# Sliding-window attention: 192 score columns per head in pieces that fit the window, in place of 256 columns and a mask

## The chip, the cores and the metric

One core of one Trainium2 chip runs the whole program. The metric is device time in microseconds (us) of one execution, from the first to the last instruction and what lies around it, as median of several executions.

## The reference

A two-layer streaming trunk: layer 0 is a gated linear recurrence with a SwiGLU FFN, layer 1 is attention with a SwiGLU FFN, and between them one shared K/V projection. The change touches the attention alone. There are 1024 prompt frames in chunks of 64, 16 query heads of 64 numbers in 4 groups, and 4 key/value heads. A query chunk sees the two chunks before it and its own, that is 192 keys, and no mask inside them:

```python
def band(a):
    ap = jnp.pad(a, ((0, 0), (WIN_CHUNKS * CHUNK, 0), (0, 0), (0, 0)))
    ...
    return jnp.concatenate([ap[:, j:j + n] for j in range(WIN_CHUNKS + 1)], axis=2)
...
m = jnp.maximum(jnp.max(s, axis=-1, keepdims=True), sink)
p = jnp.exp(s - m)
denom = jnp.sum(p, axis=-1, keepdims=True) + jnp.exp(sink - m)
return jnp.einsum('bnkgqs,bnskd->bnqkgd', p / denom, v.astype(F32))
```

Besides, 32 frames of a running stream see 128 cached keys and their own 32 (160 in all).

## The kernel before

Activations are kept feature-major in three blocks of frames (384, 384 and 288). All dense products (`mm_fm`, L132 to L142, and others like it) are done in three fp32r passes, high by high, high by low and low by high. One such product of 128 output features for one block is 24 matmuls (L141) of 128x128 weights on 384 or 288 columns, each of which the trace shows as one record.

The attention works on units of 128 queries (two chunks, a "tile") of one key/value head g with its 4 query heads (`hh = 2 * pi + pr`): 3 tiles per block, 4 groups, 3 blocks, 36 units. Tile j of 0 to 8 has 28 units with j = 1 to 7, 4 units with j = 0 (there are no keys before it) and 4 units with j = 8, the 32 sample frames. Each unit has three functions:

- `att_s` (L1249 to L1303): scores (L1272) of 128 queries against 256 keys, the four chunks that either of the two query chunks sees, for 4 heads. Operands are fp32, and each call is two matmul records in the trace. The head number pr picks the upper or the lower 64 rows of the array, because both hold 64 features of a head. Then mask products (L1282) in bf16 add a large negative number to the 64 keys that only the other chunk sees. Per half pr there is one PSUM tile `sc` of 2 heads by 256 columns, from a pool of two buffers. After that come row maxima on VectorE (L1285), the sink, the exponentials on ScalarE (L1294, with their sums), the sum's reciprocal, and the products with it: one VectorE instruction for two heads (L1299), one ScalarE instruction for each of the other two (L1302).
- `att_t` (L1305 to L1322): 8 transposes of 128x128 (L1314) through TensorE, 4 heads for each of the two key tiles, into two PSUM tiles `ptp`; ScalarE copies the first to SBUF (L1319), VectorE the second (L1321).
- `att_v` (L1324 to L1335): for each key tile two calls (L1332) of 128 keys by 64 features on 256 columns, added up in the PSUM tile `pav`, the output's upper or lower 64 partitions by pr. ScalarE rounds it to the high part (L1334), VectorE makes the low part (L1335). `ptp` and `pav` share a pool of two buffers.

The loop (L1394 to L1403) writes, for u = 0 to 12 of a block: the scores of unit u, some dense work as filling, then `att_t` and `att_v` of unit u - 1. The filling stands in `plan` (L1371 to L1381): projections of q that are left over in block 0, the output projection of block 0 in block 1, that of block 1 and the rest of block 0's in block 2. Where `plan` has nothing for a u, no dense work stands between: u = 2, 5, 8, 11 in block 0, 0, 5, 10 in block 1, and 4, 10 in block 2. A scheduler orders each engine's instructions at build time, by this order and by when it reckons that operands and buffers are ready; so dense matmuls are drawn forward into gaps, and the PE queue is then fixed. All DMAs are issued by SyncE's queue.

```python
pss = [aps.tile([128, 512], F32, tag="sc", name="sc", bufs=2)...   # L1264
ptp = aps.tile([128, 512], F32, tag="pt", name="ptp", bufs=2)      # L1312
pav = aps.tile([128, 512], F32, tag="pt", name="pav", bufs=2)...   # L1328
```

Of the kernel before, what the change touches and what calls it, by code (L numbers as in the profile page):

```python
# [29 lines left out]
NEG = -1.0e38  # L30
# [29 lines left out]
def build(nc, tc, I, O):  # L60
    ctx = ExitStack()
    mult, add, sub, mn = ALU.mult, ALU.add, ALU.subtract, ALU.min
# [20 lines left out]
    def tmp(bufs=4):  # L83
        return tp.tile([128, 384], F32, tag="tmp", name="tmp", bufs=bufs)
# [35 lines left out]
    ident = cp.tile([128, 128], F32, name="ident")  # L120
# [554 lines left out]
    def run(g):  # L675
        for _ in g or ():
            pass
# [5 lines left out]
    with tc.tile_pool(name="hp", bufs=1) as hp, \  # L683
# [42 lines left out]
        vts, o_raw, ssq, r_o = {}, {}, {}, {}  # L726
# [308 lines left out]
        p1 = p2 = None  # L1035
# [188 lines left out]
    with tc.tile_pool(name="aps", bufs=1, space=PSUM, reuse_waits="tile") as aps:  # L1224
        nsink = ap2.tile([128, 16], F32, name="nsink")
        nc.sync.dma_start(nsink, I["sinks"])
        nc.vector.tensor_scalar(nsink, nsink, -1.0, None, mult)
        mkf = tmp()
        nc.sync.dma_start(mkf, I["mk"])
        mk = ap2.tile([128, 384], BF16, name="mk")  # L1230
        nc.vector.tensor_copy(mk, mkf)
# [10 lines left out]
        def qload():  # L1242
# [3 lines left out]
            nc.sync.dma_start(qt, qds[b, g].rearrange("pi pr hf r t -> (pr hf r) pi t"))  # L1246
            qts[b, g] = qt

        def att_s(b, g, jl):  # L1249
            j = 3 * b + jl  # L1250
            samp = j == 8
            rows = 32 if samp else 128
            qs = slice(jl * 128, jl * 128 + rows)
            kb = kbs[b]
            if samp:
                keys = [(kc, 0, 128), (kb, 384, 32)]
                vals = [(vc, 128), (vts[8], 32)]
                lo, kend = 0, 160
            elif j == 0:
                keys, vals, lo, kend = [(kb, 128, 128)], [(vts[0], 128)], 128, 256  # L1260
            else:
                keys, vals, lo, kend = [(kb, jl * 128, 256)], [(vts[j - 1], 128), (vts[j], 128)], 0, 256
            rm = ap2.tile([128, 4], F32, tag="rm", name="rm", bufs=2)
            pss = [aps.tile([128, 512], F32, tag="sc", name="sc", bufs=2).rearrange("p (h k) -> p h k", h=2)  # L1264
                   for _ in range(2)]

            for pi in range(2):
                off = lo
                for (kt_, k0, n) in keys:
                    for pr in range(2):  # L1270
                        rsl = slice(pr * 64, pr * 64 + 64)
                        nc.tensor.matmul(pss[pr][:rows, pi, off:off + n], qts[b, g][rsl, pi, qs],  # L1272
                                         kt_[rsl, g, k0:k0 + n], start=pi == 0 and off == lo, stop=samp,
                                         skip_group_check=True)
                    off += n
            if not samp:
                for (c0, k0) in ((0, 128), (192, 256)):
                    if c0 < lo:
                        continue
                    for pr in range(2):  # L1280
                        rsl = slice(pr * 64, pr * 64 + 64)
# [10 lines left out]
            P = ap2.tile([128, 4, 256], F32, tag="P", name="P", bufs=2)  # L1292
            for hh in (0, 2, 1, 3):
                nc.scalar.activation(P[:rows, hh, lo:kend], pss[hh % 2][:rows, hh // 2, lo:kend], AF.Exp,  # L1294
                                     bias=ng[:rows, hh:hh + 1], scale=0.125, accum_out=rs[:rows, hh:hh + 1])
# [5 lines left out]
            for hh in (2, 3):  # L1301
                nc.scalar.activation(P[:rows, hh, lo:kend], P[:rows, hh, lo:kend], AF.Copy, scale=rs[:rows, hh:hh + 1])  # L1302
            return dict(b=b, g=g, rows=rows, qs=qs, vals=vals, lo=lo, P=P)  # L1303

        def att_t(c):  # L1305

            rows, P = c["rows"], c["P"]
            N = 4 * rows
            off = c["lo"]
            c["pt"] = []  # L1310
            for i, (vt, n) in enumerate(c["vals"]):
                ptp = aps.tile([128, 512], F32, tag="pt", name="ptp", bufs=2)  # L1312
                for hh in range(4):
                    nc.tensor.transpose(ptp[:n, hh * rows:hh * rows + rows], P[:rows, hh, off:off + n],  # L1314
                                        ident[:rows, :rows])
                off += n
                pts = ap2.tile([128, 512], F32, tag="pts", name="pts", bufs=4)
                if i == 0:
                    nc.scalar.copy(pts[:n, :N], ptp[:n, :N])  # L1319
                else:  # L1320
                    nc.vector.tensor_copy(pts[:n, :N], ptp[:n, :N])  # L1321
                c["pt"].append(pts)  # L1322

        def att_v(c):  # L1324

            rows, g, qs, vals = c["rows"], c["g"], c["qs"], c["vals"]
            oh, ol = os[c["b"]]
            pav = aps.tile([128, 512], F32, tag="pt", name="pav", bufs=2)[:, :2 * rows].rearrange("p (a q) -> p a q", a=2)  # L1328
            for i, ((vt, n), pts) in enumerate(zip(vals, c["pt"])):
                ph = pts[:n, :4 * rows].rearrange("p (pi pr q) -> p pi pr q", pi=2, pr=2)  # L1330
                for pr in range(2):
                    nc.tensor.matmul(pav[pr * 64:pr * 64 + 64], vt[:n, g * 64:g * 64 + 64], ph[:, :, pr, :],  # L1332
                                     start=i == 0, stop=i == len(vals) - 1, skip_group_check=True)
            nc.scalar.copy(oh[:, 2 * g:2 * g + 2, qs], pav)  # L1334
            nc.vector.tensor_tensor(ol[:, 2 * g:2 * g + 2, qs], pav, oh[:, 2 * g:2 * g + 2, qs].bitcast(F32), sub)  # L1335
# [4 lines left out]
        def wq(g):  # L1340
            return wpair("wq", g, scale="mix_pre1")
# [96 lines left out]
def pack(inp):  # L1438
# [35 lines left out]
    mk = np.zeros((128, 384), np.float32)  # L1474
    for r0 in (0, 64):
        mk[r0, 64:128] = 1.0
        mk[r0 + 1, 0:64] = 1.0
        mk[r0, 128:256] = NEG
        mk[r0 + 1, 256:384] = NEG
    A["mk"] = mk  # L1480
# [35 lines left out]
```

## Time and profile before

| what | value |
|---|---|
| median of 3 runs | 2513.05 us (2509.55 to 2516.27) |
| the profiled execution | 2509.75 us, of which the span is 2508.0 us |
| granted TensorE clock, mean over the span | 0.993 of full speed |
| PE busy in the span | 98% |
| the attention units, first score to last value product | about 1495 to 1742 us of the span |

PE is TensorE's matmuls, PEld its weight loads, DVE VectorE, ACT ScalarE, POOL GpSimd, SP SyncE. A matmul's record lasts longer than it holds up the next one, since matmuls are pipelined: how long a group keeps the engine is read from its start to the start of the next group. "x8" counts records that follow each other, and the us ahead of it run from the first start to the last end.

### The profile page before, as it was taken

What the parts mean: (1) busy time and instruction counts of PE and PEld (TensorE: products, weight loads), DVE (VectorE), ACT (ScalarE), POOL (GpSimd) and SP (SyncE); (2) the same over time, 40 slices, a digit from 0 to 9 for tenths busy, and PEclk for the clock granted to TensorE, in tenths of its full rate; (3) what the DMA queues carried; (4) which work ended last, traced back from release to release, by engine and by line L of the source; (5) the groups of instructions that cost most, each with busy time, mean ns of one, the idle gap of its engine ahead of it and who ended that gap; (6) DMA issues with size and microseconds to landing.
All of it is one profiled execution on the core that took longest, in us unless ns stands there. A gap on an engine that the chain in (4) does not pass through costs nothing.

```text
span 2508.0 us, 43904 instructions
## 1 busy us (share of the span) xinstructions
PE 2455.1 (98%) x17124; PEld 2367.2 (94%) x17124; DVE 1707.5 (68%) x3678; ACT 1130.2 (45%) x2467; POOL 243.3 (10%) x476
## 2 busy tenths in 40 slices
PE   7999999999999999999999999999999999999997
PEld 7999998998999999999999997778999999999997
DVE  8888889888876666652468746678876666643466
ACT  6655655656533333342345326677533333341333
POOL 3343233231000000000000211000000000000000
PEclk9999999999999999999999999999999999999999
DMA  5233334443522222252446532233422222242454
GB/s 177 91 102 102 122 105 133 134 136 106 165 71 86 76 77 76 75 173 81 145 145 204 177 123 71 86 117 102 156 74 77 77 77 77 76 168 77 153 168 157
DMA packets 124153, 287.98 MB, mean 115 GB/s; under 512 B 13432, under 2 KB 68632, under 8 KB 123944
## 3 DMA queue, kind: packets, MB, share of 16 engines
q1 hardware_dynamic: 123944, 285.17, 35.0%
q8 instruction: 134, 2.20, 0.4%
q14 instruction: 75, 0.61, 0.1%
HBM read 237.25 MB, written 48.07 MB: 114 GB/s over the span
## 4 chain that ended last, share of the span: by engine, by line
PE 79%; DVE 10%; DMA 5%; ACT 4%; issue 2%; POOL 1%; SPq 0%; DVEq 0%; ACTq 0%; POOLq 0%
PE mm L141 27%; PE mm L507 17%; PE mm L416 15%; PE mm L153 6%; PE c L416 6%; PE sc L1272 2%; DVE wl L103 2%; PE pav L1332 1%; PE ptp L1314 1%; DMA wst<-in_wfo 1%; ACT wh L102 1%; DVE acc L182 1%; DVE wl L99 1%; DMA xl<-g 1%; DMA wst<-in_wk 1%
## 5 line engine op out<-in xcount | busy, mean ns | idle before, releaser
L141 PE MATMUL mm<-xh,wh 128*128 128x384 f32 (+1 forms) x1968 | 630.4, 321 | 10.4 <-ACT xh L220 7.0
L141 PE MATMUL mm<-xh,wl 128*128 128x384 f32 (+1 forms) x1968 | 622.2, 317 | 4.2 <-DVE wl L103 4.2
L141 PE MATMUL mm<-xl,wh 128*128 128x384 f32 (+1 forms) x1968 | 623.2, 317 | 0.2
L102 ACT CAST wh<-wst 128x1024 fp32r<-128x1024 f32 (+1 forms) x301 | 314.3, 1047 | 365.5 <-PE mm L507 196.5
L103 DVE TENSOR_TENSOR wl<-wst,wh 128x1024 fp32r<-128x1024 f32 (+1 forms) x301 | 368.1, 1226 | 137.7 <-ACT wh L102 137.3
L141 PEld LDWEIGHTS mm<-xh,wh 128*128 128x128 f32 x1968 | 371.2, 189 | 19.5 <-ACT xh L220 7.0
L141 PEld LDWEIGHTS mm<-xh,wl 128*128 128x128 f32 x1968 | 371.7, 189 | 10.6 <-DVE wl L103 6.2
L141 PEld LDWEIGHTS mm<-xl,wh 128*128 128x128 f32 x1968 | 371.5, 189 | 8.7 <-issue 5.0
L507 PE MATMUL mm<-xh,wl 128*128 128x384 f32 (+1 forms) x768 | 247.3, 322 | 2.4 <-DVE wl L103 2.4
L507 PE MATMUL mm<-xh,wh 128*128 128x384 f32 (+1 forms) x768 | 247.3, 322 | 0.0
L507 PE MATMUL mm<-xl,wh 128*128 128x384 f32 (+1 forms) x768 | 247.2, 322 | 0.0
L153 PE MATMUL mm<-wh,xh 128*128 128x256 f32 (+1 forms) x648 | 188.1, 290 | 3.9 <-DVE tmp L1130 2.5
L153 PE MATMUL mm<-wh,xl 128*128 128x256 f32 (+1 forms) x648 | 184.5, 285 | 0.0
L153 PE MATMUL mm<-wl,xh 128*128 128x256 f32 (+1 forms) x648 | 184.3, 284 | 0.0
L400 ACT CAST sh<-sr 128x512 fp32r<-128x512 f32 x144 | 89.5, 622 | 173.8 <-PE mm L416 145.6
L507 PEld LDWEIGHTS mm<-xh,wl 128*128 128x128 f32 x768 | 144.9, 189 | 2.8 <-DVE wl L103 2.8
L507 PEld LDWEIGHTS mm<-xl,wh 128*128 128x128 f32 x768 | 144.8, 189 | 0.0
L507 PEld LDWEIGHTS mm<-xh,wh 128*128 128x128 f32 x768 | 144.7, 188 | 0.0
L153 PEld LDWEIGHTS mm<-wh,xh 128*128 128x128 f32 (+1 forms) x648 | 119.2, 184 | 6.7 <-DVE tmp L1130 2.6
L153 PEld LDWEIGHTS mm<-wh,xl 128*128 128x128 f32 (+1 forms) x648 | 119.3, 184 | 0.8 <-issue 0.2
L153 PEld LDWEIGHTS mm<-wl,xh 128*128 128x128 f32 (+1 forms) x648 | 119.5, 184 | 0.6
L399 DVE TENSOR_TENSOR sr<-wst 128x512 f32<-128x512 f32 x72 | 49.5, 688 | 74.9 <-DMA wst<-in_wfi 74.9
(284 smaller groups left out, 5115.7 us busy)
## 6 DMA issues: line engine op xcount, KB each, us to landing
wst<-in_wfo SPq DMA_DIRECT2D x92, 512.0 KB
wst<-in_wfi SPq DMA_DIRECT2D x88, 512.0 KB
wst<-in_wfq SPq DMA_DIRECT2D x47, 512.0 KB
g<-u SPq DMA_DIRECT2D x72, 192.0 KB
wst<-in_wi SPq DMA_DIRECT2D x24, 512.0 KB
wst<-in_wg SPq DMA_DIRECT2D x24, 512.0 KB
wst<-in_wao SPq DMA_DIRECT2D x24, 512.0 KB
xl<-g SPq DMA_DIRECT2D x32, 384.0 KB
```

Of the source, the lines that this page charges most:

```text
L99: nc.vector.scalar_tensor_tensor(wl[:, s], st[:, s], pcol(name, k0 + k), wh[:, s].bitcast(F32), mult, sub)
L102: nc.scalar.copy(wh[:, s], st[:, s])
L103: nc.vector.tensor_tensor(wl[:, s], st[:, s], wh[:, s].bitcast(F32), sub)
L141: last_mm[0] = nc.tensor.matmul(ps[:, :W], w, x, start=i == 0, stop=i == n - 1)
L153: last_mm[0] = nc.tensor.matmul(ps[:rows, :256], x, w, start=i == 0, stop=i == n - 1)
L182: nc.vector.tensor_tensor(acc[:, :W], acc[:, :W], q[:, :W], add)
L399: nc.vector.tensor_tensor(r, x, y, op)
L400: nc.scalar.copy(h, r)
L416: last_mm[0] = nc.tensor.matmul(ps[:, :384], a, c, start=start and k == i == 0, stop=k == 3 and i == 2, skip_group_check=True)
L507: last_mm[0] = nc.tensor.matmul(ps[:, :W], a, c[:, q, :], start=start and q == i == 0, stop=stop and q == f - 1 and i == 2, skip_group_che ...
L1272: nc.tensor.matmul(pss[pr][:rows, pi, off:off + n], qts[b, g][rsl, pi, qs], kt_[rsl, g, k0:k0 + n], start=pi == 0 and off == lo, stop=samp ...
L1314: nc.tensor.transpose(ptp[:n, hh * rows:hh * rows + rows], P[:rows, hh, off:off + n], ident[:rows, :rows])
```

## The change

A tile's two query chunks 2j and 2j+1 have 128 keys in common (chunks 2j-1 and 2j) and 64 alone each (chunk 2j-2, and chunk 2j+1). The scores are made so: the common keys for all 128 queries (64 rows by 128 columns of the array, 128 moving columns), then each chunk's own keys in a quarter of the array (64 rows by 64 columns, 64 moving columns, one quarter for each pair of pr and chunk). A head has 192 score columns, and the mask products, their constant and its DMA go. Columns lie as common, own, own, common for pi = 0 and 1, so that one transpose takes the own keys of both pi: 6 transposes in place of 8. For the value product the common keys need V rows of two half tiles in 128 partitions: `shift` makes these copies `sv` by DMA (16 DMAs and one memset in all, on SyncE's queue and GpSimd). The value product is 4 calls of 128 columns on the common keys and 8 calls of 64 columns in quarters on the own keys. `sc` becomes one PSUM tile of two banks with one buffer, and `ptp` and `pav` share one of two banks with one buffer. For j = 0 VectorE's memsets write the missing columns in PSUM (4 in each of 4 units).

```diff
-        mk = ap2.tile([128, 384], BF16, name="mk")
...
+        def shift(j):
+            svs[j] = ap2.tile([128, 256], F32, tag="sv", name="sv", bufs=6)
+            if j == 0:
+                nc.gpsimd.memset(svs[0][0:64], 0.0)
+            else:
+                nc.sync.dma_start(svs[j][0:64], vts[j - 1][64:128])
+            if j < 8:
+                nc.sync.dma_start(svs[j][64:128], vts[j][0:64])
...
-            pss = [aps.tile([128, 512], F32, tag="sc", name="sc", bufs=2).rearrange("p (h k) -> p h k", h=2)
-                   for _ in range(2)]
+            ps = aps.tile([128, 2, 512], F32, tag="sc", name="sc", bufs=1)
+            cc, oc = (0, 256), (128, 384 - n)
+            def mm(pr, pi, p0, m, c0, keys, k0, w):
+                rsl = slice(pr * 64, pr * 64 + 64)
+                q0 = jl * 128 + p0
+                nc.tensor.matmul(ps[p0:p0 + m, pr, c0:c0 + w], qts[b, g][rsl, pi, q0:q0 + m],
+                                 keys[rsl, g, k0:k0 + w], start=True, stop=True, skip_group_check=True)
...
+                    elif j == 0:
+                        mm(pr, pi, 0, 128, cc[pi] + 64, kb, 128, 64)
+                    else:
+                        mm(pr, pi, 0, 128, cc[pi], kb, k0 + 64, 128)
             if not samp:
-                for (c0, k0) in ((0, 128), (192, 256)):
...
-                        nc.tensor.matmul(pss[pr][:, :, c0:c0 + 64], mk[rsl, 0:128], mk[rsl, k0:k0 + 128], start=False,
-                                         stop=True, skip_group_check=True)
+                for pi in range(2):
+                    for p0, c0 in ((0, 0), (64, 192)):
+                        if j > 0 or p0:
+                            for pr in range(2):
+                                mm(pr, pi, p0, 64, oc[pi], kb, k0 + c0, 64)
+            if j == 0:
+                for pr in range(2):
+                    nc.vector.memset(ps[:, pr, 0:384].rearrange("p (i k) -> p i k", i=3)[:, 0:3:2, 0:64], NEG)
+                    nc.vector.memset(ps[0:64, pr, 128:256], NEG)
             for pr in range(2):
-                nc.vector.tensor_reduce(rm[:rows, pr:4:2], pss[pr][:rows, :, lo:kend], AX.X, ALU.max)
+                nc.vector.tensor_reduce(rm[:rows, pr:4:2], sc[:rows, pr], AX.X, ALU.max)
...
-            nc.vector.tensor_tensor(P[:rows, 0:2, lo:kend], P[:rows, 0:2, lo:kend],
-                                    rs[:rows, 0:2].unsqueeze(2).broadcast_to([rows, 2, kend - lo]), mult)
...
+            for pi in range(2):
+                o = pi * (384 - n)
+                nc.vector.tensor_scalar(P[:rows, 0, o:o + n], P[:rows, 0, o:o + n], rs[:rows, 2 * pi:2 * pi + 1], None,
+                                        mult)
+                nc.scalar.activation(P[:rows, 1, o:o + n], P[:rows, 1, o:o + n], AF.Copy,
+                                     scale=rs[:rows, 2 * pi + 1:2 * pi + 2])
...
+            pt = aps.tile([128, 2, 512], F32, tag="pt", name="ptp", bufs=1)
...
+                    nc.tensor.transpose(t1[:, pr, pi, :rows], P[:rows, pr, 256 * pi:256 * pi + 128], idt)
...
+                    nc.tensor.transpose(t2[:, pr], P[:, pr, 128:256], idt)
+                nc.scalar.copy(p1, t1)
+                nc.vector.tensor_copy(p2, t2)
...
+            pav = aps.tile([128, 2, 512], F32, tag="pt", name="pav", bufs=1)
+            for pi in range(2):
                 for pr in range(2):
+                    nc.tensor.matmul(pav[pr * 64:pr * 64 + 64, pi, :rows], (vc if j == 8 else svs[j])[:, fs],
+                                     p1[:, pr, pi, :rows], start=True, stop=False, skip_group_check=True)
...
+                for ch in range(2):
+                    vs = ((vts[j - 1], svs[j - 1]) if ch == 0 else (svs[j + 1], vts[j])) if j + ch else ()
+                    cs = slice(ch * 64, ch * 64 + 64)
+                    for pr in range(2):
+                        for pi, vt in enumerate(vs):
+                            hs = slice(pi * 64, pi * 64 + 64)
+                            nc.tensor.matmul(pav[pr * 64:pr * 64 + 64, pi, cs], vt[hs, fs], p2[hs, pr, cs],
+                                             start=False, stop=True, skip_group_check=True)
...
         run(vproj1(2, uv))
+        for j in range(4):
+            shift(j)
...
             os[b] = newx(b)
+            for j in range(3 * b + 1, min(9, 3 * b + 4)) if b else ():
+                shift(j)
```

## Rows read from the trace of the kernel before

**Rows 1.** The page's part 1, and the chain that ended last, by engine.

```profile
PE 2455.1 (98%) x17124; PEld 2367.2 (94%) x17124; DVE 1707.5 (68%) x3678; ACT 1130.2 (45%) x2467; POOL 243.3 (10%) x476
PE 79%; DVE 10%; DMA 5%; ACT 4%; issue 2%; POOL 1%; SPq 0%; DVEq 0%; ACTq 0%; POOLq 0%
```

**Rows 2.** Windows, first and last block of the attention: us, busy by engine, clock, DMA, GB/s.

```profile
1490.00:1570.00 80.00, 79.14 (x519) 61.63 (x520) 50.05 (x124) 45.63 (x157) 9.47 (x10) 1.00 0.26 77
...
1660.00:1742.00 82.00, 81.53 (x565) 62.65 (x564) 69.86 (x169) 64.76 (x204) 0.00 (x0) 1.00 0.37 120
```

**Rows 3.** Waits in 1490 to 1745: who waited for whom, total us, times, longest.

```profile
PEld pav L1332 <- ACT pts L1319: 8.1, 23, 0.8
```

**Rows 4.** Timeline of PE around one unit's scores and mask products.

```profile
1611.34 0.34 PE L141 MATMUL mm<-xh,wl 128*128 128x384 f32 x1
1611.52 0.33 PE L141 MATMUL mm<-xh,wh 128*128 128x384 f32 x1
1611.78 1.14 PE L1272 MATMUL sc<-kb,qt 64*128 64x256 f32 x8
1612.75 0.28 PE L1282 MATMUL sc<-mk 64*128 64x128 bf16 x4
1612.96 0.45 PE L141 MATMUL mm<-xl,wh 128*128 128x384 f32 x1
1613.24 0.34 PE L141 MATMUL mm<-xh,wl 128*128 128x384 f32 x1
```

**Rows 5.** Timeline of PE around the 8 transposes of a unit.

```profile
1614.48 1.03 PE L1314 MATMUL ptp<-ident,P 128*128 128x128 f32 x8
1615.28 0.42 PE L141 MATMUL mm<-xh,wh 128*128 128x384 f32 x1
1615.53 0.34 PE L141 MATMUL mm<-xl,wh 128*128 128x384 f32 x1
```

**Rows 6.** Timeline of PE and PEld around a unit's value products.

```profile
1618.10 0.63 PEld L1332 LDWEIGHTS pav<-pts,vt 128*64 128x64 f32 x8 [0.33 <-ACT pts L1319]
1618.11 1.08 PE L1332 MATMUL pav<-pts,vt 128*64 128x256 f32 x8
1619.12 0.28 PE L1282 MATMUL sc<-mk 64*128 64x128 bf16 x4
```

**Rows 7.** Timeline of PE in layer 0: matmuls in quarters and halves by columns.

```profile
499.59 0.53 PE L913 MATMUL psA<-XX,K 128*32 128x80 f32 x17
...
500.42 0.55 PE L927 MATMUL psB<-ZZ,K 128*64 128x96 f32 x8
500.81 0.39 PE L930 MATMUL psB<-Q,K 128*64 128x64 f32 x4
501.13 0.39 PE L153 MATMUL mm<-wh,xh 128*128 128x256 f32 x1
```

**Rows 8.** Timeline of PE: half of a unit's value products; scores half after half.

```profile
1529.26 0.65 PE L1332 MATMUL pav<-pts,vt 128*64 128x256 f32 x4
1529.84 0.44 PE L141 MATMUL mm<-xh,wh 128*128 128x384 f32 x1
...
1588.34 2.04 PE L1272 MATMUL sc<-kb,qt 64*128 64x256 f32 x8
```

**Rows 9.** Groups by shape, 1490 to 1745: busy us, mean ns, idle before.

```profile
L1294 ACT ACTIVATE P<-sc,ng 128x256 f32<-128x256 f32 x112 | 51.5, 472 | 23.6 <-DVE ng L1290 22.1 <-issue 1.5
L1294 ACT ACTIVATE P<-sc,ng 128x128 f32<-128x128 f32 x16 | 5.7, 365 | 1.6 <-DVE ng L1290 1.6
L1285 DVE TENSOR_REDUCE rm<-sc 128x2 f32<-128x512 f32 x56 | 36.4, 680 | 1.5 <-PE sc L1282 1.4
L1285 DVE TENSOR_REDUCE rm<-sc 128x2 f32<-128x256 f32 x8 | 3.3, 420 | 8.1 <-PE sc L1282 8.1
```

**Rows 10.** Timeline: the next unit's scores after rows 4, and a DMA's issue.

```profile
1616.16 0.73 PEld L1272 LDWEIGHTS sc<-kb,qt 64*128 64x128 f32 x4 [0.26 <-ACT P L1294]
1700.91 0.33 SPq L91 DMA_DIRECT2D wst<-in_wbo  x1
```

More of the change, by code (lines that the diff above doesn't have):

```diff
@@ L1247, in qload @@
             qts[b, g] = qt
+        svs = {}
+        def shift(j):
[6 more added lines that the diff above has]
+                nc.sync.dma_start(svs[j][64:128], vts[j][0:64])
         def att_s(b, g, jl):
@@ L1251, in att_s @@
             samp = j == 8
-            rows = 32 if samp else 128
-            qs = slice(jl * 128, jl * 128 + rows)
+            rows, n = (32, 160) if samp else (128, 192)
             kb = kbs[b]
[L1255 to L1262, printed above, removed]
@@ L1263, in att_s @@
-            rm = ap2.tile([128, 4], F32, tag="rm", name="rm", bufs=2)
-            pss = [aps.tile([128, 512], F32, tag="sc", name="sc", bufs=2).rearrange("p (h k) -> p h k", h=2)
-                   for _ in range(2)]
-            for pi in range(2):
[L1268 to L1275, printed above, removed]
@@ L1291, in att_s @@
             nc.vector.tensor_tensor(es[:rows], ng[:rows], nsg, sub)
-            P = ap2.tile([128, 4, 256], F32, tag="P", name="P", bufs=2)
+            P = ap2.tile([128, 2, 384], F32, tag="P", name="P", bufs=2)
             for hh in (0, 2, 1, 3):
-                nc.scalar.activation(P[:rows, hh, lo:kend], pss[hh % 2][:rows, hh // 2, lo:kend], AF.Exp,
+                pi, pr = hh // 2, hh % 2
+                nc.scalar.activation(P[:rows, pr, pi * (384 - n):pi * (384 - n) + n], sc[:rows, pr, pi], AF.Exp,
                                      bias=ng[:rows, hh:hh + 1], scale=0.125, accum_out=rs[:rows, hh:hh + 1])
@@ L1305, in att_t @@
+            return dict(b=b, g=g, j=j, rows=rows, qs=slice(jl * 128, jl * 128 + rows), P=P)
         def att_t(c):
             rows, P = c["rows"], c["P"]
[L1308 to L1322, printed above, removed]
+            pt = aps.tile([128, 2, 512], F32, tag="pt", name="ptp", bufs=1)
@@ new lines, in att_t @@
+            c["p1"] = p1 = ap2.tile([128, 2, 2, 128], F32, tag="p1", name="p1", bufs=2)
+            c["p2"] = p2 = ap2.tile([128, 2, 128], F32, tag="p2", name="p2", bufs=2)
+            t1 = pt[:, 0].rearrange("p (r i q) -> p r i q", r=2, i=2)
+            t2 = pt[:, 1, 0:256].rearrange("p (r q) -> p r q", r=2)
+            idt = ident[:rows, :rows]
+            for pr in range(2):
+                for pi in range(2):
+                    nc.tensor.transpose(t1[:, pr, pi, :rows], P[:rows, pr, 256 * pi:256 * pi + 128], idt)
@@ new lines, in att_t @@
+            if rows == 32:
+                for pr in range(2):
+                    for pi in range(2):
+                        nc.tensor.transpose(t2[:32, pr, pi * 32:pi * 32 + 32], P[:32, pr, 128 + 96 * pi:160 + 96 * pi], idt)
+                nc.scalar.copy(p1[:, :, :, :32], t1[:, :, :, :32])
+                nc.vector.tensor_copy(p2[:32, :, :64], t2[:32, :, :64])
+            else:
+                for pr in range(2):
+                    nc.tensor.transpose(t2[:, pr], P[:, pr, 128:256], idt)
+                nc.scalar.copy(p1, t1)
+                nc.vector.tensor_copy(p2, t2)
@@ L1324, in att_v @@
         def att_v(c):
-            rows, g, qs, vals = c["rows"], c["g"], c["qs"], c["vals"]
+            rows, g, j, qs, p1, p2 = c["rows"], c["g"], c["j"], c["qs"], c["p1"], c["p2"]
             oh, ol = os[c["b"]]
-            pav = aps.tile([128, 512], F32, tag="pt", name="pav", bufs=2)[:, :2 * rows].rearrange("p (a q) -> p a q", a=2)
-            for i, ((vt, n), pts) in enumerate(zip(vals, c["pt"])):
-                ph = pts[:n, :4 * rows].rearrange("p (pi pr q) -> p pi pr q", pi=2, pr=2)
+            fs = slice(g * 64, g * 64 + 64)
@@ L1331, in att_v @@
+            pav = aps.tile([128, 2, 512], F32, tag="pt", name="pav", bufs=1)
+            for pi in range(2):
                 for pr in range(2):
[L1332 to L1335, printed above, removed]
+                    nc.tensor.matmul(pav[pr * 64:pr * 64 + 64, pi, :rows], (vc if j == 8 else svs[j])[:, fs],
+                                     p1[:, pr, pi, :rows], start=True, stop=False, skip_group_check=True)
@@ new lines, in att_v @@
+            if j == 8:
+                for pi in range(2):
+                    for pr in range(2):
+                        nc.tensor.matmul(pav[pr * 64:pr * 64 + 64, pi, :32], vts[8][:32, fs], p2[:32, pr, pi * 32:pi * 32 + 32],
+                                         start=False, stop=True, skip_group_check=True)
+            else:
+                for ch in range(2):
+                    vs = ((vts[j - 1], svs[j - 1]) if ch == 0 else (svs[j + 1], vts[j])) if j + ch else ()
+                    cs = slice(ch * 64, ch * 64 + 64)
+                    for pr in range(2):
+                        for pi, vt in enumerate(vs):
+                            hs = slice(pi * 64, pi * 64 + 64)
+                            nc.tensor.matmul(pav[pr * 64:pr * 64 + 64, pi, cs], vt[hs, fs], p2[hs, pr, cs],
+                                             start=False, stop=True, skip_group_check=True)
@@ L1337, in op1 @@
+            nc.scalar.copy(oh[:, 2 * g:2 * g + 2, qs], pav[:, :, :rows])
+            nc.vector.tensor_tensor(ol[:, 2 * g:2 * g + 2, qs], pav[:, :, :rows],
+                                    oh[:, 2 * g:2 * g + 2, qs].bitcast(F32), sub)
         def op1(b):
@@ L1473, in pack @@
     A["msk"] = _masks()
[L1474 to L1480, printed above, removed]
     pos = np.concatenate([np.arange(NP), 256 + np.arange(NS)]).astype(np.float32)
```

15 lines of the change are left out of this document (5 added, 10 removed).

## Prediction

> **What bounds it now.** I read the page first: PE is busy 98% of the span and carries 79% of the chain that ended last [rows 1]. So only what shortens PE's queue, or makes PE wait, can move the time. The stretch that the change touches runs from about 1495 to 1742 us, 247 us for 36 units. In the windows of its blocks PE is busy 79.14 of 80 us and 81.53 of 82, at a granted clock of 1.00 (2.4 GHz), while VectorE has 70 of 82 us at most and ScalarE 65 [rows 2]. A busy PE can hide waits, since records are drawn until their matmul ends, so I looked at the waits: the largest that ends on attention data, value products on the copied transposes, is 8.1 us in 23 pieces [rows 3]. So in these 247 us PE is the bound, and its queue is read by slots, from the start of one group to the start of the next.
>
> **Prices from the rows.** A 64-column fp32 matmul record holds its part of the array for about 0.055 us: four of them and a change to full-array work take 0.32 us, of which 0.10 is the change [rows 7]. That is 0.86 ns a column, so 0.11 us for 128 columns and 0.22 for 256. Eight records of 256 columns in two halves of the rows take 0.97 us [rows 4]: four slots of 0.22 and 0.09 for the first weight load, which nothing covers. So the halves run side by side. So do halves by columns: eight records of 256 columns in 1.01 us [rows 6], eight of 96 in 0.39 [rows 7]. Changing the shape costs twice. The engine empties: the dense matmul at 1611.52 should hand over after 0.17 us (its own step from 1611.34 is 0.18), yet the scores start 0.26 us later, so 0.09 is lost. And the first load is bare: 0.09 to 0.10 for 128 columns (the first dense matmul after the mask keeps its slot 0.28 us in place of 0.17 [rows 4]), 0.05 for 64 columns (rows 6: 1.01 less 4 x 0.22 less the 0.09 of emptying).
>
> **Part by part, one full unit (28 of 36).**
> Scores: now 0.97 + 0.21 for the mask products, 1.18 us with the emptying behind them [rows 4]. After: the common keys are 8 records of 128 columns in two halves, 0.09 + 4 x 0.11 = 0.53; a change to quarters, 0.09 + 0.05; the own keys are 16 records of 64 columns in four quarters, 4 x 0.055 = 0.22; emptying 0.09. Sum 0.98, which saves 0.20.
> Transposes: 8 keep PE from 1614.48 to 1615.53 less the dense matmul's 0.17, 0.88 us or 0.11 each [rows 5]. Six save 0.22.
> Value products: now 1.01 us [rows 6]. After: 0.05 + 4 x 0.11 = 0.49, change and bare load 0.14, quarters 0.22, emptying 0.09, in all 0.94. Saves 0.07.
> Together 0.49 us, and 28 x 0.49 = 13.7 us, all on PE and so on the path.
>
> The quarters are the unknown: no row of before has a matmul in a quarter of 64 rows by 64 columns. Bounds: four abreast, 0.22 for a group of 16 (halves by rows and by columns each run side by side, and 17 records in four quarters by columns all lie in 0.53 us, where in series they would need 17 x 0.07 = 1.2 [rows 7]); one after the other, 16 x 0.055 = 0.88. I take 0.22, since both kinds of halves are shown and the four column quarters too. By the pace of those 17 (0.53 / 17 = 0.031 at most) 16 would need 0.50, which is too dear as it counts the last one's whole record. The Trainium skill, page "TensorE: Matmul & The Clock Gate", section "Wait — 56ns, not 53.3ns?", has matmuls never start closer than about 25 ns; by that a group would take at least 0.40 us, and the estimate's gain would fall by 56 x 0.18 = 10 us to under 4. No run here shows such a floor: 8 records of two halves in 0.97 us neither show nor exclude it.
>
> Units of j = 0 (4): fewer keys now (scores in two pieces, 4 transposes, half the value product), 6 transposes after; 2 more transposes (+0.22) against the mask products and one visit less (about -0.3): nothing. Their 16 memsets on VectorE cost an estimated 0.2 us each, beside dense PE work; if that cover is gone, 0.8 us in each of 4 units, 3 us. Sample units (4) keep their work; +0.1 each for the second shape, 0.4 us.
> ScalarE and VectorE: exponentials of 192 columns in place of 256 take 0.42 by the two shapes' 0.47 and 0.37, row maxima 0.55 in place of 0.68 [rows 9], the DVE copy half as much. This is nothing on the path, since neither bounds; it shortens the way from scores to probabilities by some 0.5 us.
> DMAs: 16 small copies on SyncE's queue at 0.33 us of issue [rows 10], 5 us over some 200, and the mask's DMA goes. They copy V rows made long before; the three at the start of block 1 stand near the k load, and the scheduler's queue order decides who waits. PE's dense work covers them: nothing, and at most some 2 us once if a value product of block 1's first unit waited.
>
> Sum: 13.7 - 0.4 = 13.3 us; I say 13.5 with the trifles of the first unit's mask DMA. The profiled execution's 2509.75 becomes 2496; the runs' median 2513.05 stands 3.3 us above it, so 2499.5 is my number. On the better side two things add: value products that now come in two visits of 4 records, 0.58 each (1529.26 to 1529.84) plus a second dense re-entry of 0.10, 1.27 in all [rows 8], would be 1.04, another 0.16 for some half of the units, 2 us; and scores whose second half waits for its buffer run half after half, 2.04 us in place of 1.14 [rows 8], some five times, 5 us. Then 21 us are saved.
>
> **Rivals.**
> A. Slower: weight loads in quarters don't hide. A quarter's load of 64 columns (0.05) is as long as its matmul, and two quarters share the same rows. If a load could not run under a matmul in its rows, each row half would take 8 loads and 8 matmuls in series, 0.88 us for a group in place of 0.27: 0.61 x 56 groups = 34 us, net 20 slower, 2534. It decides from 0.51 us a group on (13.5 / 56 = 0.24 above 0.27). Against: eight loads of the value products are all begun and done within 0.63 us, under matmuls of the same 128 rows that run to 1619.12 [rows 6]; in series they would make 0.88 + 8 x 0.05 + 0.09 = 1.4 us, not 1.01. For: never seen with rows and columns cut at once. The same page of the Trainium skill, section "Part 3: Packing small matmuls — row/col tiling", says that weight loads overlap matmuls in flight "only when row_grp differs", which is this case; rows 6 contradict it for column halves. Chance 0.08.
> B. Quarters two abreast, or a floor between starts: 0.44 a group, 0.22 x 56 = 12 us, net 1 us faster, about 2512, the same. Chance 0.10.
> C. A new wait: `sc` with one buffer lets no score start until all four exponentials of the unit before are through, where now the first half starts after two (1616.16, on an exponential, 4.4 us after 1611.78) [rows 4, 10]; and a transpose waits until the last value product is copied out. The loop after: 0.9 scores, 1.1 maxima, 0.3 sink, 1.6 exponentials and handovers, some 4.1 us. A unit has 247 / 36 = 6.9 us on average, but nine units have no filling in the plan and only 2.6 us of attention: 1.5 x 9 = 14 us of waits if no dense work is drawn forward, and the time stays at about 2513. Against: today's loop is 4.4 to 5.3 us against 3.1 of work in the same units, which would give 15 us of waits, and the rows show few [rows 2, 3]: dense matmuls were drawn forward. Chance 0.14.
> D. The clock falls more often, since emptying leaves PE idle more often. At 1.00 throughout these blocks [rows 2]; 0.02, to "same".
>
> **Numbers.** Forecast 0.66. A measurement of this kernel tells changes over 0.3%, 7.5 us, from none: faster is below 2505.5. The forecast's own range, 8 to 21 us saved, is 2492 to 2505. With B and C the range reaches to 2514; at the low end 4 us more for what the scheduler packs better, 2488. Left out are A and the tails. Faster 0.66, same 0.25, slower 0.09.
>
> **What would show it.** In a full unit the group of own scores, 16 records of 64x64, should hold PE about 0.27 us from its first start, and six transposes 0.65; the stretch from first score to last value product should shrink from 247 to some 234 us, with the rest of the span unchanged. Groups at 0.5 or 0.9 speak for B or A; a growth of PE's idle time before scores on the exponentials, or before transposes on the rounding of `pav`, for C. I am wrong if the stretch is not shorter by 8 us, or if the time moves elsewhere.

## The result and the profile after

| what | before | after |
|---|---|---|
| median of 5 runs each, on one chip in turn | 2510.73 us (2509.55 to 2516.27) | 2499.08 us (2498.28 to 2503.11) |
| ratio, 95% interval | | 0.9946 (0.9934 to 0.9958) |
| profiled execution, its span | 2509.75, 2508.0 us | 2499.08, 2496.6 us |
| first score to last value product | 246.8 us | 229.1 us |
| end of layer 0 to first FFN matmul of layer 1 | 485.3 us | 468.4 us |

The number came out as forecast: 2499.5 us was said, 2499.08 measured. (The two medians of five alone lie 11.7 us apart, a ratio of 0.9954; the ratio in the table stands for 13.6 us, and 13.5 was forecast.) The way to it did not, and the profile shows where to look. First the page's part 1 and the chain by engine, as in [rows 1]:

```profile
PE 2426.9 (97%) x17964; PEld 2361.4 (95%) x17964; DVE 1695.8 (68%) x3733; ACT 1124.0 (45%) x2467; POOL 245.5 (10%) x477
PE 74%; DVE 12%; DMA 6%; ACT 5%; issue 2%; POOL 1%; SPq 0%; DVEq 0%; ACTq 0%; POOLq 0%
```

PE's share of the chain fell from 79% to 74%, VectorE's rose from 10 to 12 and the DMAs' from 5 to 6: a little of the path has left TensorE. The windows of the attention's three blocks (columns as in [rows 2]) say the same:

```profile
1490.00:1570.00 80.00, 77.58 (x786) 68.32 (x787) 50.39 (x147) 40.71 (x141) 12.96 (x12) 1.00 0.29 82
1570.00:1660.00 90.00, 88.51 (x1030) 73.70 (x1031) 62.64 (x181) 69.04 (x225) 0.00 (x0) 1.00 0.35 99
1660.00:1735.00 75.00, 68.68 (x763) 58.11 (x763) 64.52 (x175) 60.12 (x194) 0.00 (x0) 0.98 0.39 123
```

In the last block PE is idle for 6.3 of 75 us, where it was idle for 0.5 of 82 [rows 2]. Now the timeline of PE around one unit, to set against [rows 4 to 6]:

```profile
1611.47 1.11 PE L1273 MATMUL sc<-kb,qt 64*128 64x128 f32 x24
1612.51 0.66 PE L1333 MATMUL ptp<-ident,P 128*128 128x128 f32 x4
1613.00 0.38 PE L1342 MATMUL ptp<-ident,P 128*128 128x128 f32 x2
...
1614.54 0.66 PE L1355 MATMUL pav<-p,sv 128*64 128x128 f32 x8
1615.13 0.27 PE L1370 MATMUL pav<-p,vt 64*64 64x64 f32 x1
1615.13 0.27 PE L1370 MATMUL pav<-p,sv 64*64 64x64 f32 x1
1615.14 0.27 PE L1370 MATMUL pav<-p,vt 64*64 64x64 f32 x1
1615.15 0.27 PE L1370 MATMUL pav<-p,sv 64*64 64x64 f32 x1
1615.23 0.22 PE L1370 MATMUL pav<-p,vt 64*64 64x64 f32 x1
...
1615.52 0.44 PE L141 MATMUL mm<-xh,wh 128*128 128x384 f32 x1
```

From start to start the scores keep PE 1.04 us (1611.47 to 1612.51; 0.98 was forecast), the six transposes 0.63 (1612.51 to 1613.14, where the next dense matmul starts; 0.65 was forecast), the value products 0.98 (0.94). The 16 own products of a group start four at a time, 6 or 7 ns apart. In most groups 0.39 us pass from the first of them to the start of other work; less the 0.09 of emptying that is about 0.30, where 0.27 was forecast: four quarters abreast, and neither rival A's 0.88 nor B's 0.44. So the prices were good. What they were multiplied with was not. These are the records of the scores' line alone, PE's busy time from 1490 to 1760 us (then PEld's, clock, DMA share, GB/s), of the kernel before:

```profile
1490.00:1760.00 270.00, 57.65 (x320) 35.50 (x320) 0.99 0.31 96
```

and of the kernel after:

```profile
1490.00:1760.00 270.00, 41.07 (x800) 31.56 (x800) 0.99 0.38 113
```

The prediction's 0.20 us for 28 units would be 5.6 us of scores with the mask products in it. These records alone, without the masks, lost 16.6.

Now the whole stretch between layer 0 and the FFN as one window (columns as in [rows 2]), before and after:

```profile
1373.41:1858.72 485.31, 477.13 (x3111) 415.45 (x3110) 347.51 (x767) 269.68 (x755) 37.35 (x38) 0.99 0.37 115
1377.25:1845.61 468.36, 448.79 (x3952) 410.26 (x3951) 336.56 (x824) 263.29 (x755) 39.48 (x40) 0.99 0.40 122
```

PE's busy time there fell by 28.3 us, twice what was forecast, but its idle time grew from 8.2 to 19.6 us. In the table each matmul record counts from its start to the start of the next one, less the time in which no record runs, which is the idle time. The forecast is 28 times what the prediction saved in a unit:

| PE's time in the stretch, us | before | after | change | forecast |
|---|---|---|---|---|
| scores and mask products | 58.9 | 38.7 | -20.2 | -5.6 |
| transposes | 29.0 | 22.2 | -6.8 | -6.2 |
| value products | 35.5 | 33.6 | -1.9 | -2.0 |
| dense work | 353.7 | 354.3 | +0.6 | 0 |
| idle | 8.2 | 19.6 | +11.4 | 0 |

So the stretch got only some 17 us shorter. Most of the new idle time, 8.3 of 11.4 us, lies between 1480 and 1760 us. Who waited for whom there (total us, times, longest):

```profile
PE mm L188 <- DVE acc L182: 3.7, 1, 3.7
PE pav L1355 <- DVE p L1344: 2.3, 5, 1.0
PE ptp L1333 <- DVE P L1316: 1.6, 4, 0.6
PEld pav L1355 <- DVE p L1344: 4.4, 15, 0.6
PEld sc L1273 <- ACT es L1310: 3.2, 14, 0.3
```

The dearest, 3.7 us, is no attention at all. The next are value products (L1355) that wait for the copied probabilities and transposes (L1333) that wait for the normalised ones. Timelines of VectorE and PE around it:

```profile
1706.95 1.20 DVE L103 TENSOR_TENSOR wl<-wst,wh 128x1024 fp32r<-128x1024 f32 x1
...
1708.67 1.15 DVE L278 SCALAR_TENSOR_TENSOR xo<-xo,pv,rb 128x384 f32<-128x384 f32 x2 [0.52 <-DMA xo<-xsc]
...
1709.81 0.55 DVE L182 TENSOR_TENSOR acc<-acc,tmp 128x384 f32<-128x384 f32 x1
...
1710.42 1.57 PE L188 MATMUL mm<-acc,ones 128*128 128x384 f32 x2 [3.72 <-DVE acc L182]
```

Block 0's residual is loaded back by DMA (L275) into `xo`, which has two buffers. VectorE waits 0.52 us for it and then works 1.15 us on what was loaded; the norm's sum stands behind that in VectorE's queue, and PE waits for the sum. So the load itself is 0.5 of the 3.7 us; before it VectorE was busy, the last 1.20 us with the low part of weights (L103). Afterwards the granted clock is 0.51 (1.2 GHz) from 1710.5 to 1714.

One caution on the profiles: layer 0 is the same program in both, and took 1373.4 us before and 1377.3 after (1372.1 to 1380.8 in the profiles of all kernels below). So the spans differ by 11.4 us where the stretch differs by 16.9.

### The profile page after: what moved, and what is told of

Read it like the earlier page. It is cut to its first block, busy times and chain, and to the rows that moved or that the text cites. A ratio compares the mean times of both kernels' runs of the same rounds, so it can differ in the third digit from the quotient of the medians.

```text
span 2496.6 us, 45627 instructions
## 1 busy us (share of the span) xinstructions
PE 2426.9 (97%) x17964; PEld 2361.4 (95%) x17964; DVE 1695.8 (68%) x3733; ACT 1124.0 (45%) x2467; POOL 245.5 (10%) x477
## 4 chain that ended last, share of the span: by engine, by line
PE 74%; DVE 12%; DMA 6%; ACT 5%; issue 2%; POOL 1%; SPq 0%; DVEq 0%; ACTq 0%; POOLq 0%
PE mm L141 25%; PE mm L507 18%; PE mm L416 15%; PE c L416 6%; PE mm L153 5%; DVE wl L103 2%; ACT wh L102 1%; DMA wst<-in_wfo 1%; DVE wl L99 1%; PE sc L1273 1%; DMA wst<-in_wfq 1%; DVE acc L182 1%; PE pav L1355 1%; DMA xl<-g 1%; DMA wst<-in_wk 1%
## 5 line engine op out<-in xcount | busy, mean ns | idle before, releaser
L103 DVE TENSOR_TENSOR wl<-wst,wh 128x1024 fp32r<-128x1024 f32 (+1 forms) x301 | 369.2, 1230 | 137.8 <-ACT wh L102 136.4
L99 DVE SCALAR_TENSOR_TENSOR wl<-wst,pv,wh 128x256 fp32r<-128x256 f32 x160 | 78.7, 528 | 35.2 <-ACT wh L98 34.8
```

The source lines that it names most:

```text
L99: nc.vector.scalar_tensor_tensor(wl[:, s], st[:, s], pcol(name, k0 + k), wh[:, s].bitcast(F32), mult, sub)
L103: nc.vector.tensor_tensor(wl[:, s], st[:, s], wh[:, s].bitcast(F32), sub)
```

## The experiments

Theory 1 is the prediction's: the gain is slots on TensorE, as narrower pieces take fewer. Theory 2: the gain is the softmax, whose row maxima and exponentials on 192 columns shorten the way from scores to probabilities. Ratios are against runs of the kernel before on the same chip.

**e1: part of TensorE's saving given back.** The own keys' transposes run twice.

```diff
-                for pr in range(2):
+                for pr in (0, 1, 0, 1):
                     nc.tensor.transpose(t2[:, pr], P[:, pr, 128:256], idt)
```

> The changed kernel, but the two transposes of the own keys are done twice in each of the 32 full and first units (the same values are written again). Theory 1, TensorE's slots set the time of the attention: 32 x 2 x 0.11 = 7.0 us more than the changed kernel, some 2506 us, ratio to the kernel before about 0.997. Theory 2, the shorter softmax on VectorE and ScalarE made the gain and TensorE has room: no change, some 2499 us, ratio 0.9946.

2501.31 us, ratio 0.9957 (0.9945 to 0.9969): of 7.0 us some 2.8 arrive. The two theories' values, about 0.997 and 0.9946, lie at the two ends of the interval, so the time alone refutes neither. The profile is plainer: counted as in the table, the transposes grew by 7.4 us, and PE's idle time shrank from 19.6 to 15.5. That fits PE being the bound for part of the time.

**e2: the softmax's saving given back.** One more row maximum and one more exponential per unit, unused.

```diff
+            if j < 8:
+                dm = ap2.tile([128, 4], F32, tag="dm", name="dm", bufs=1)
+                nc.vector.tensor_reduce(dm[:rows, 0:2], sc[:rows, 1], AX.X, ALU.max)
...
+            if j < 8:
+                nc.scalar.activation(ps[:rows, 1, 384:512], sc[:rows, 1, 1, 0:128], AF.Exp, bias=ng[:rows, 3:4], scale=0.125)
```

> The changed kernel with work added on the way from scores to probabilities in each of the 32 full and first units: one more row maximum of 384 columns on VectorE (0.55 us) and one more exponential of 128 columns on ScalarE (about 0.27 us of slot), results unused; about what 192 in place of 256 columns saved there. Theory 1, TensorE's slots: at most 2 us more than the changed kernel, 2499 to 2501 us, ratio 0.994 to 0.996. Theory 2, the shorter softmax made the gain: most of the 11.6 us is lost, 2507 to 2511 us, ratio 0.998 to 1.000.

2508.62 us, 0.9977 (0.9968 to 0.9986): over half of the gain is gone with no change in PE's work. PE's idle time rose from 19.6 to 24.1 us; among the waits, 1490 to 1745 us:

```profile
PEld sc L1273 <- ACT sc L1314: 5.7, 13, 1.2
PEld pav L1360 <- DVE p L1349: 5.6, 9, 1.7
```

The scores wait for the extra exponential (L1314 here) to free their one buffer, the value products for the copy of the transposed probabilities. So this loop does stand close behind PE. The edit adds some 0.9 us to it, though, where the change saved about half as much, so it overstates what the saving brought.

**e3: own scores chunk after chunk.** Only the order in which they are called.

```diff
-                for pi in range(2):
-                    for p0, c0 in ((0, 0), (64, 192)):
+                for p0, c0 in ((0, 0), (64, 192)):
+                    for pi in range(2):
```

> The changed kernel with the own-key scores called for one chunk after the other (both pi of the first chunk, then both of the second), so that only the two row halves are neighbours in the queue. If quarters run side by side only where they are neighbours in the queue: the group of 16 takes about 0.44 to 0.50 us in place of 0.27, 28 x 0.2 = 5 to 6 us more, about 2505 us, ratio 0.997. If TensorE finds them anywhere in its queue: no change, 2499 us, ratio 0.9946, and the group's length stays.

2501.72 us, 0.995 (0.9936 to 0.9964), no change. In the timeline of PE the group is as long as before:

```profile
1614.31 1.12 PE L1273 MATMUL sc<-kb,qt 64*128 64x128 f32 x24
```

**e4: block 0's residual loaded back into `tmp`'s four buffers,** not `xo`'s two.

```diff
-                    if full == "back":
-                        v = tt("xo", 2)[:, :W]
+                    if full in ("back", "back1"):
+                        v = (tt("xo", 2) if full == "back" else tmp())[:, :W]
```

> The changed kernel, but the rows of block 0 that are loaded back in layer 1 go to the four tmp buffers in place of the two xo buffers. In the changed kernel TensorE stands still for 3.7 us near the end of the attention, for an accumulation on VectorE that is queued behind a product waiting for such a load, and its clock is then at half for 3.4 us. If the two buffers hold up the loads: the wait and the slow window go, 3.7 + 1.7 = 5 us less, about 2494 us, ratio 0.9925. If the load waits for its data or the queue: no change, 2499 us, or a wait for tmp buffers elsewhere.

2496.66 us, 0.9933 (0.992 to 0.9945), the lowest ratio of all, though the interval overlaps the change's. The wait of 3.72 us became, in the timeline of PE:

```profile
1707.54 1.65 PE L188 MATMUL mm<-acc,ones 128*128 128x384 f32 x2 [1.32 <-DVE acc L182]
```

So a wait remains, and the stretch is no shorter in the profiles, 468.9 us against 468.4.

**e5: the shorter softmax in the kernel before.** Row maxima, exponentials and normalising on 192 of 256 columns, with zeros from GpSimd in the other 64, which are left out of the computation (as in e12). The same bound stands at each of these lines:

```diff
+            ke = min(kend, lo + 192)
...
-                nc.vector.tensor_reduce(rm[:rows, pr:4:2], pss[pr][:rows, :, lo:kend], AX.X, ALU.max)
+                nc.vector.tensor_reduce(rm[:rows, pr:4:2], pss[pr][:rows, :, lo:ke], AX.X, ALU.max)
...
+            if ke < kend:
+                nc.gpsimd.memset(P[:rows, :, ke:kend], 0.0)
```

> The kernel before, with all its matrix products, but row maxima, exponentials and the products with the reciprocal sum go over 192 of a head's 256 columns; the last 64 are left out (GpSimd writes zeros there). Theory 1, TensorE's slots alone set the time of the kernel before: no change, ratio 0.999 to 1.001. Theory 2, the way through VectorE and ScalarE set it: 6 to 9 us less, ratio 0.9965 to 0.9975. With the run of the changed kernel with the softmax work given back (2508.6 us, ratio 0.9977) this makes a table of two by two.

2508.06 us, 0.998 (0.997 to 0.9991), between the two. Nothing was taken from PE, yet PE's busy time on the scores' line fell from 57.65 us:

```profile
1490.00:1760.00 270.00, 50.37 (x320) 29.24 (x320) 0.99 0.34 103
```

These are the same 320 records of the same shapes. Of the 224 with 256 columns, 150 start in pairs; before, 100 do. Something else than their size sets what the scores cost.

**e6: the first four shifts after the last projection,** away from the load of q's weights.

```diff
-        for j in range(4):
-            shift(j)
...
         run(qproj(0, 3, uq3))
+        for j in range(4):
+            shift(j)
```

> The changed kernel with the DMAs that copy V rows for the first four tiles written after the last projection ahead of the attention, in place of right behind the V projection. In the changed kernel nine of them hold SyncE's queue for 4.9 us at 1437 to 1445 us, and the loads of the next weights behind them come later. If that delays the projections: 2 to 4 us less than the changed kernel, ratio 0.993 to 0.9938. If the loads wait for their buffers anyway: no change, 0.9946.

2496.4 us, 0.9946 (0.9928 to 0.9963). In the change nine copies of 0.48 to 0.60 us each stand on SyncE's queue from 1437 to 1445, ahead of a weight load, as its timeline shows:

```profile
1438.21 0.59 SPq L1255 DMA_DIRECT2D sv<-vt  x1
1438.85 0.59 SPq L1253 DMA_DIRECT2D sv<-vt  x1
...
1447.09 0.43 SPq L91 DMA_DIRECT2D wst<-in_wq  x1
```

Moving them changes nothing that can be told. **e8, e4 and e6 together:**

> The changed kernel with two of the edits together: the rows loaded back go to the tmp buffers (alone 0.9933), and the copies of V rows are issued late. If their gains add: 5 to 7 us less than the changed kernel, ratio 0.992. If one makes the other idle: 0.993.

2498.35 us, 0.9942 (0.9928 to 0.9956): they don't add up, and it is not told apart from the change.

**e7: the scores in two tiles of one bank with two buffers,** as before, and all else as in the change.

```diff
-            ps = aps.tile([128, 2, 512], F32, tag="sc", name="sc", bufs=1)
+            pss = [aps.tile([128, 512], F32, tag="sc", name="sc", bufs=2) for _ in range(2)]
```

> The changed kernel with the scores in two PSUM tiles of one bank with two buffers, as in the kernel before, so that a half's scores can start when its own two exponentials are through. If the single buffer holds up the scores: 2 to 5 us less than the changed kernel, ratio 0.9925 to 0.994. If it doesn't: no change, 0.9946. If the halves come one after the other again and no quarters run abreast: 3 to 5 us more, 0.996.

2513.49 us, 1.0001 (0.9992 to 1.0011). The whole gain is gone, which neither theory had. The scores' line alone, and PE's timeline of one group:

```profile
1490.00:1760.00 270.00, 61.57 (x800) 47.91 (x800) 0.98 0.34 101
```

```profile
1612.76 1.99 PE L1273 MATMUL sc<-kb,qt 64*128 64x128 f32 x24
```

61.57 us where the change has 41.07 for the same 800 records, and a group of 1.99 us where it has 1.11. Inside it the common keys' products start one at a time, by their count those of one row half and then those of the other. PE is not idle between them: it is the queue's order. Counted over the attention, 212 of the 224 records of 128 columns in the change start in pairs, within 20 ns of each other; here 76 do. The reading, argued and not shown: with a buffer for each half the build-time scheduler places one half as soon as it reckons that half's buffer free, while with one tile both become ready together and stand in turns, as they are called.

**e9: only that tile, in the kernel before.**

```diff
-            pss = [aps.tile([128, 512], F32, tag="sc", name="sc", bufs=2).rearrange("p (h k) -> p h k", h=2)
-                   for _ in range(2)]
+            ps2 = aps.tile([128, 2, 512], F32, tag="sc", name="sc", bufs=1)
+            pss = [ps2[:, pr].rearrange("p (h k) -> p h k", h=2) for pr in range(2)]
```

> The kernel before with its scores in one PSUM tile of two banks and one buffer, in place of two tiles of one bank and two buffers; nothing else is changed. Theory S (the common tile is what keeps the two row halves abreast, worth the whole of the 13.5 us that e7 lost): the scores before ran half after half in part of the units, so these become abreast and the kernel gets faster by some 5 us, ratio 0.998, with the slots of its scores down from 49.4 us toward 28 x 1.06 + 10 = 40. Rival (rival C of the prediction: one buffer makes the first half wait for all four exponentials): 256 columns make that loop longer than in the change, so no change or slower, 1.000 to 1.003. Should it bring as much as e7 lost (0.9946), the change's narrower pieces would be worth nothing by themselves.

2506.26 us, 0.997 (0.9957 to 0.9983): over half of the change's gain with none of its narrower pieces. The scores' line, 57.65 us before:

```profile
1490.00:1760.00 270.00, 41.95 (x320) 24.75 (x320) 0.99 0.33 101
```

and PE's timeline in the stretch in which the kernel before has the 2.04 us of [rows 8]:

```profile
1580.22 1.13 PE L1272 MATMUL sc<-kb,qt 64*128 64x256 f32 x8
1587.89 1.13 PE L1272 MATMUL sc<-kb,qt 64*128 64x256 f32 x8
1594.29 1.14 PE L1272 MATMUL sc<-kb,qt 64*128 64x256 f32 x8
1600.68 1.14 PE L1272 MATMUL sc<-kb,qt 64*128 64x256 f32 x8
```

Of 224 records 212 start in pairs, where 100 did. If all of the 112 more had run alone before, sharing their time saves 112 x 0.11 = 12 us, and the units come in 39 pieces in place of 54, which spares the emptying: 15.7 us on this line. Half of what PE saves comes back as waiting: its busy time in the stretch fell by 10.7 us, from 477.1 to 466.4, and its idle time grew from 8.2 to 13.4.

**e10: the kernel before without its mask products,** which leaves the mask out.

```diff
-                                         kt_[rsl, g, k0:k0 + n], start=pi == 0 and off == lo, stop=samp,
+                                         kt_[rsl, g, k0:k0 + n], start=pi == 0 and off == lo, stop=True,
...
-            if not samp:
+            if False:
```

> The kernel before with its mask products left out and nothing else changed: the probabilities of the 64 keys that only the other chunk sees are not masked, so the output differs. The mask products hold TensorE for 11.0 us of slots in the profile of before. If every slot on TensorE counts in full: 11 us less, ratio 0.9956. If only the part counts that e1 showed for added slots (about 0.4): 4.4 us less, 0.998. If nothing counts, as the softmax sets the pace: 1.000.

2518.7 us, 1.0016 (1.0007 to 1.0025): slower, by 4 us, with the 11.0 us of mask slots taken out. None of the three forecasts holds. The scores' line stays at 58.20 us, so the halves are still apart. But PE's busy time in the stretch is 477.1 us in both kernels: scores and masks lost 4.5 us, the transposes, value products and dense work gained as much, and the idle time grew from 8.2 to 14.9. PE also ran at half the clock (0.52) for some 10 us from 1726, which by itself costs some 4 us, an estimate from the 8.3 us in which PE was busy there. What the queue's new order did in detail was not settled. So the run took no time from PE after all, and it can't say what such time is worth.

**e11: e8 with the own keys' transposes and their copy first.**

```diff
+            if rows > 32:
+                for pr in range(2):
+                    nc.tensor.transpose(t2[:, pr], P[:, pr, 128:256], idt)
```

> The change, with block 0's rows loaded back into the four buffers of tmp (e4), the first four shifts after the last projection (e6), and in each unit the two transposes of the own keys ahead of the four of the common keys, so that VectorE's copy of them, on which the last eight value products wait, starts earlier. If the waits of value products on that copy (1.45 us at 1731, 1.2 us at 1517 in the change) count on the path: 2 to 4 us less than e8, ratio 0.993 or less. If they are covered by other work: as e8, 0.994.

The two copies change places with them. 2508.06 us, 0.9978 (0.9967 to 0.9988), some 9 us worse than e8. The common keys' transposes now come later, and so does their copy (L1345 here), on which the first value products wait. Waits from 1480 to 1760 us:

```profile
PEld sc L1273 <- ACT P L1308: 6.5, 7, 2.9
PEld pav L1356 <- ACT p L1345: 6.1, 21, 1.4
```

**e12: e9 and e5 together.**

> The kernel before with the edits of e9 and e5 together: scores in one tile of two banks and one buffer, and row maxima, exponentials and normalising on 192 of 256 columns (the other 64 probabilities are written as zeros by GpSimd, so 64 columns are left out of the computation). TensorE still makes 256 columns, the mask products, 8 transposes and the wide value products. If the common tile and the shorter softmax are what the change gains, this stands as the change does, 0.9935 to 0.9955, and the narrower pieces on TensorE are worth nothing beside them. If the narrower pieces are worth what the prediction says beyond that, it stays where e9 is, 0.996 to 0.998, as the shorter softmax has nothing left to shorten. The slots of scores and mask products should stand at e9's 44 us by either.

2505.67 us, 0.9967 (0.9956 to 0.9977): as e9. The slots of scores and masks stand at 48.4 us, though, and not at the 44 that were expected; e9 has 43.9. With the halves side by side the shorter softmax brings nothing on top that can be told. That e5's 5 us were the same gain by another way fits, as fewer score records ran alone there, but it is argued.

The four corners, then: neither edit 1; the common tile alone 0.997, with the shorter softmax 0.9967; narrower pieces and shorter softmax without the tile 1.0001; with it 0.9946. The tile is worth some 7.5 us, and the narrower pieces some 5 more (0.9967 to 0.9946, whose intervals just overlap), but only with the tile. In the profiles the stretch is 485.3 us before, 479.7 in e9, 478.5 in e12 and 468.4 in the change, which gives the narrower pieces the larger part. So about half of the gain is the tile's; which half is larger is open.

## Why the number was right and its reasons only half

**The prices held.** Quarters run four abreast, their loads are hidden, and 1.04, 0.63 and 0.98 us stand against 0.98, 0.65 and 0.94. Rivals A and B were false. The prediction's remark that 8 records in two halves "neither show nor exclude" a floor between starts read its rows too coarsely: in the trace of before, records of two row halves that make a pair start 6 to 19 ns apart, 28 of the 50 pairs 6 or 7. Exponentials and row maxima took what two shapes of before gave, in the groups by shape:

```profile
L1308 ACT ACTIVATE P<-sc,ng 128x192 f32<-128x192 f32 x128 | 52.3, 424 | 12.7 <-DVE ng L1303 11.2 <-PE pav L1370 1.4
L1298 DVE TENSOR_REDUCE rm<-sc 128x2 f32<-128x384 f32 x64 | 33.2, 550 | 8.1 <-PE sc L1273 7.8
```

**The step that failed** is the scores' "now 0.97 + 0.21", read from one unit [rows 4] and multiplied by 28. In that unit the halves ran together; over the attention 124 of 224 records did not start in a pair, and 80 of them had no other within 0.2 us. That form stood in [rows 8] and was booked as "some five times, 5 us" on the better side; by e9 it was 15.7 us. Scores and masks fell by 20.2 us where 5.6 was forecast, 14.6 more; transposes and value products came out as forecast. One view would have told: PE's busy time on the scores' line over the whole attention is 57.65 us, and 28 units at the 1.14 of [rows 4] are 31.9, to which eight short units cannot add 26. And `sc` in one tile was read as a risk (rival C), when it was about half of the gain.

**The second step that failed** is "all on PE and so on the path". PE's busy time fell by 28.3 us, and the stretch by 16.9; the other 11.4 are idle time. That is close to the 14 us that rival C priced, but not where C put it: the scores' loads wait for the exponentials no longer than before (3.2 us for L1310 and 1.1 for L1308, before 1.8 and 2.9 for L1296 and L1294), and transposes wait for the rounding of `pav` 1.4 us in all. PE now reaches transposes, value products and the norm's sum before VectorE has them ready. e1's profile shows it from one side (7.4 us more of transposes, 4.1 less of idle time), e2 and e11 from the other. So two errors, 14.6 us too little on the scores and 11.4 us of waits put at nothing, had opposite signs and nearly cancelled: that the sum came out is luck.

**Smaller terms.** "Nothing on the path" for the softmax was right where PE is long (e12 against e9). Where PE has become short e2 speaks against it, though e2 adds more than the change saved. Rival C's loop adds up to 3.9 us by its own terms, not 4.1, which gives 12 us of waits in place of 14. The memsets of j = 0 took 0.165 us each, 0.2 being the estimate. The shifts took 0.46 to 0.60 us of SyncE's queue each, not 0.33; the stretch from layer 0's end to the first score grew from 121.5 to 125.4 us, but e6 does not show that they are to blame. D, the clock: 0.98 to 1.00 in the three blocks, with half-speed stretches after the longest waits, as 3.4 us from 1710.5.

**Open** are the order within e10's queue, and whether forcing the halves to stand in turns with two buffers would beat the one tile; that was not tried. Nor does any run test alone that `ptp` and `pav` now share a single buffer: by the code the first value products must wait until both copies of the transposed probabilities are through, and their loads wait 4.4 us in all for the second of them (L1344). e4 has the lowest ratio measured, 0.9933, but it is not told apart from the change with certainty.

## What to carry to other kernels

A price read from one group is a price for all only when the line's total over the stretch says so: multiply out, and compare with the busy time of that line alone. Products that are to run side by side in the array want operands and buffers that become ready together; a buffer for each half, which looks like more freedom, let the order split them here, and cost the change its whole gain. And where TensorE is 98% busy with a softmax loop close behind, time taken from it turns in part into waits, so each microsecond saved there is to be weighed against the loop that comes next.

## What the runs showed of the hardware

Matmuls in different quarters of 64 rows by 64 columns start 6 or 7 ns apart, four at a time, and 16 of them hold the engine about 0.30 us. By the floor of about 25 ns between starts that the Trainium skill gives (page "TensorE: Matmul & The Clock Gate", section "Wait — 56ns, not 53.3ns?") they would have needed 0.40, an estimate; the trace speaks against it across quarters.

The loads of two quarters in the same rows hide as well, or 16 products could not pass in 0.30 us. A rule listed on the same page of the Trainium skill, section "Part 3: Packing small matmuls — row/col tiling", lets a weight load overlap a matmul only where the row group differs; these groups, with two quarters in each row half, contradict it, as [rows 6] did for column halves.

Records of half the array that start alone take 0.22 us each for 256 columns, and a pair of them takes the same 0.22. That was known from the rows; that it was worth about as much here as all that makes the pieces narrower was not.
